# Gate and up products of a two-layer hybrid decoder: hi and lo parts of the transposed input as one 512-column operand, in blocks of 128 weight columns

## The chip, the cores and the metric

The kernel runs on one core of one Trainium2 chip. The metric is the device time of one execution in microseconds (us), lower is better. A profile is one execution recorded by the hardware profiler; its span runs from the first instruction to the last. In the profile PE is the matrix engine (TensorE), PEld its weight loads, DVE the vector engine, ACT the scalar (activation) engine, POOL the GpSimd engine and SP the engine that issues DMAs.

## What is computed

Two layers run over all 256 positions at once, with a model width of 1024 and an FFN width of 2816, all in float32. Each layer has an FFN, a mixer and a second FFN:

```python
def swiglu(x, w_gate_up, w_down):
    gate, up = jnp.split(x @ w_gate_up, 2, axis=-1)
    return (jax.nn.silu(gate) * up) @ w_down

for l in range(DEPTH):
    x = x + FFN_HALF * swiglu(rms_norm(x, ffn1_norm[l]), ffn1_w_gate_up[l], ffn1_w_down[l])
    u = rms_norm(x, mix_norm[l]) @ w_in[l]
    ...
    x = x + y @ w_out[l]
    x = x + FFN_HALF * swiglu(rms_norm(x, ffn2_norm[l]), ffn2_w_gate_up[l], ffn2_w_down[l])
return rms_norm(x, final_norm)
```

The mixer between the FFNs joins three sequence mixers (a state-space one, an mLSTM and an RWKV-7). The change does not touch its computation.

## The kernel before

**Precision by splitting.** The matrix engine works on a rounded 32-bit type (`F32R`). To keep float32 accuracy each operand is split in two: `hi` is the operand copied to `F32R`, `lo` is the rest (operand minus `hi`). A product is then three matmuls into the same bank of PSUM: hi by hi, hi by lo, lo by hi. `mm3` (lines 804 to 808) issues these three, so L806, L807 and L808 carry nearly all matrix work. Weights are split on the chip in `weights` (L773 on ACT makes hi, L774 on DVE makes lo), and activations in `split_to` (L824, L825).

**The FFN (`ffn`, line 956).** The FFN width is cut in `NG` = 11 groups of 256. The transposed, split input is held by `Turned` as two tensors, `hi` and `lo`, each 128 partitions by 8 chunks by 256 positions. Group 0 is made by `first_up` in another layout (the positions are the stationary operand and 512 weight columns move), and `turn` transposes its result. The scale of the norm comes as a row `R` from `rows`. Groups 1 to 10 are made by `gate_up` (line 1004): the weights are the stationary operand, 128 columns at a time, and the 256 positions move. For each of 8 chunks, of gate and up, and of the two halves `b` of the 256 columns one `mm3` is issued:

```python
mm3(banks[g][:, b * T:(b + 1) * T], (wh[:, k, g, b, :], wl[:, k, g, b, :]), hT(kk),
    kk == 0 and b == 0, kk == 7)
```

This is 8 x 2 x 2 x 3 = 96 matmuls of 256 columns for a group, into two banks of 512 columns. Then five steps on 512 columns follow: gate times R (L1025, DVE), Silu (L1026, ACT), times up (L1027, DVE), and the split (L824 ACT, L825 DVE). Between two groups stands `down` (line 1030) for the group before: per block of 128 FFN rows and per half `t` of the positions, 2 x 3 matmuls with 512 moving weight columns, that is 24 for a group, into four banks kept through the whole FFN (`acc`). In the last group `down` is done for positions 0 to 127 first; the next stage's `tile(0)` starts from them (residual add L834, squares L838, transposes L870 and their splits L873, L874, or L865 with L824, L825 before a mixer), while the other half's products run.

**Weights.** They come in pieces of 128 partitions by 1024 floats (512 KB), in the order of `specs`: for each FFN group four pieces of gate and up columns (`spec_gu`, each two DMAs, rows of 256 floats, 1 KB) and two pieces of down rows (`spec_rows`, rows of 4 KB). The mixer's `spec_cols` pieces have rows of 128 floats, 512 bytes.

**What sets the order.** Every operation is first recorded and then placed by a list scheduler (`Planner`, lines 158 to 587), which emits a fixed order per engine. `cost` (line 292) gives each operation an estimated occupancy; for `F32R` matmuls it is 0.46 ns per moving column. `run` (line 358) takes the operation that can start earliest; on PE the recorded order of the dense matmuls breaks ties. It assigns places in SBUF and the eight PSUM banks; three classes of bank have caps: `acc` 4, `main` 3 (gate and up, projections, transposes of the input), `task` 5 (the mixers' own). Pieces of weights are split early when their first use is near.

Of the kernel before, what the change touches and what calls it, by code (L numbers as in the profile page):

```python
# [21 lines left out]
F32 = mybir.dt.float32  # L22
# [135 lines left out]
class Planner:  # L158
# [133 lines left out]
    def cost(self, op, outs, ins):  # L292
# [65 lines left out]
    def run(self, reserve, wmin, wmax, urgent, keep_max, spare):  # L358
# [232 lines left out]
def kernel(ctx: ExitStack, tc: tile.TileContext, x, pvec, prow, fnorm, w_gate,  # L591
# [256 lines left out]
    class Turned:  # L848


        def __init__(self):
            self.hi, self.lo = (newr(8 * T).rearrange("p (k t) -> p k t", k=8) for _ in range(2))

        def __call__(self, k, t=None):
            ts = slice(0, T) if t is None else slice(t * 128, (t + 1) * 128)
            return self.hi[:, k, ts], self.lo[:, k, ts]

        def fill(self, t, src, gain=None):

            ts = slice(t * 128, (t + 1) * 128)  # L860
            if gain is None:
                for h in range(2):
                    bv = mmb().rearrange("p (k c) -> p k c", k=4)
                    for k in range(4):
                        pe.transpose(bv[:, k, :], src(h)[:, k * 128:(k + 1) * 128], ident)  # L865
                    split_to(self.hi[:, h * 4:h * 4 + 4, ts], self.lo[:, h * 4:h * 4 + 4, ts], bv)
                return
            bv = [b.rearrange("p (k c) -> p k c", k=4) for b in (mmb(), mmb())]
            for k in range(8):
                pe.transpose(bv[k % 2][:, k // 2, :], src(k // 4)[:, k % 4 * 128:(k % 4 + 1) * 128], ident)  # L870
            for k in range(8):
                v, g = bv[k % 2][:, k // 2, :], gain[:, k:k + 1]
                act.activation(out=self.hi[:, k, ts], in_=v, func=AF.Copy, scale=g)  # L873
                dve.scalar_tensor_tensor(out=self.lo[:, k, ts], in0=v, scalar=g, in1=self.hi[:, k, ts].bitcast(F32),  # L874
                                         op0=ALU.mult, op1=ALU.subtract)

    class ToFfn:

# [77 lines left out]
    def ffn(inp, update, make_next, first=None):  # L956
# [2 lines left out]
        pts = {}  # L959
        hT = inp.hT  # L960

        def pt_pair(j):
            pts[j] = newr(512), newr(512)
            return pts[j]

        def gated(ps, s, p, t):

# [16 lines left out]
        def turn(p):  # L984
            with ranked(1):
                b = mmb()
                bv = b.rearrange("p (k t c) -> p k t c", k=2, t=2)
                for t in range(2):
                    for k in range(2):
                        pe.transpose(bv[:, k, t, :], p[:, t * 256 + k * 128:t * 256 + (k + 1) * 128], ident)  # L990
                split_to(*pt_pair(0), b)

        def rows():

# [8 lines left out]

        def gate_up(j, R):

            banks = [mmb(), mmb()]
            for i in range(4):
                (w,) = weights(1)
                wh, wl = (v.rearrange("p (k g b c) -> p k g b c", k=2, g=2, b=2) for v in w[1:])
                with dense(w):  # L1010
                    for k in range(2):
                        kk = 2 * i + k
                        for g in range(2):
                            for b in range(2):

                                mm3(banks[g][:, b * T:(b + 1) * T], (wh[:, k, g, b, :], wl[:, k, g, b, :]), hT(kk),
                                    kk == 0 and b == 0, kk == 7)
            with ranked(1):
                s = new(512)
                hi, lo = pt_pair(j)  # L1020
                gate, up, sv, hv, lv = (v.rearrange("p (b c) -> p b c", b=2) for v in (*banks, s, hi, lo))
                for ts in ((slice(0, T),) if j < NG - 1 else (slice(0, 128), slice(128, T))):
                    n = ts.stop - ts.start
                    v = sv[:, :, ts]
                    dve.tensor_tensor(out=v, in0=gate[:, :, ts], in1=R[:, None, ts].to_broadcast([128, 2, n]), op=ALU.mult)  # L1025
                    act.activation(out=v, in_=v, func=AF.Silu)  # L1026
                    dve.tensor_tensor(out=v, in0=up[:, :, ts], in1=v, op=ALU.mult)  # L1027
                    split_to(hv[:, :, ts], lv[:, :, ts], v)

        def down(j, k, t, w, hs=(0, 1)):  # L1030
            hi, lo = pts[j]
            o = (k * 2 + t) * 128
            with dense(w):
                for h in hs:
                    mm3(acc[t][h], (hi[:, o:o + 128], lo[:, o:o + 128]),
                        (w[1][:, h * 512:(h + 1) * 512], w[2][:, h * 512:(h + 1) * 512]),
                        j == 0 and k == 0, j == NG - 1 and k == 1)

        p = first_up()
        if first is not None:  # L1040
            first()
        R = rows()
        for j in range(1, NG):
            gate_up(j, R)
            if acc is None:
                acc = [[accb(), accb()], [accb(), accb()]]
            if j == 1:
                turn(p)
            if j < NG - 1:
                for k in range(2):  # L1050
                    (w,) = weights(1)
                    down(j - 1, k, 0, w)
                    down(j - 1, k, 1, w)
            else:
                wa = weights(2)
                for k in range(2):
                    down(j - 1, k, 0, wa[k])
                wb = weights(2)
                for h in range(2):
                    for k in range(2):  # L1060
                        down(j, k, 0, wb[k], (h,))
                nxt = make_next()
                nxt.tile(0, (acc[0], inp.half[0]))
                for hs in nxt.tail:
                    for k in range(2):
                        down(j - 1, k, 1, wa[k], hs)
                    for k in range(2):
                        down(j, k, 1, wb[k], hs)
        return nxt, (acc[1], inp.half[1])


# [832 lines left out]
```

## Time and profile before

| what | value |
|---|---|
| time, median of 3 runs (lowest, highest) | 1304.84 us (1300.2, 1305.63) |
| profiled execution, its own time | 1305.16 us |
| its span, mean granted clock of PE | 1303.4 us, 0.990 |
| matmuls in it | 9170 |
| weight loads' busy share (PEld) | 88% |
| DVE, ACT, POOL busy share | 62%, 49%, 7% |
| DMA traffic | 210.35 MB, mean 161 GB/s |

How to read it: a matmul's duration in the profile reaches from its start to the modelled end of its pipeline, so that consecutive matmuls overlap in time and a busy PE need not be a PE at its peak. What a matmul costs in a dense stream is the distance from its start to the next one's start, called its pitch here. Busy times of a group of rows are unions, so overlapping records are not counted twice.

### The profile page before, as it was taken

What the parts mean: (1) busy time and instruction counts of PE and PEld (TensorE: products, weight loads), DVE (VectorE), ACT (ScalarE), POOL (GpSimd) and SP (SyncE); (2) the same over time, 40 slices, a digit from 0 to 9 for tenths busy, and PEclk for the clock granted to TensorE, in tenths of its full rate; (3) what the DMA queues carried; (4) which work ended last, traced back from release to release, by engine and by line L of the source; (5) the groups of instructions that cost most, each with busy time, mean ns of one, the idle gap of its engine ahead of it and who ended that gap; (6) DMA issues with size and microseconds to landing.
All of it is one profiled execution on the core that took longest, in us unless ns stands there. A gap on an engine that the chain in (4) does not pass through costs nothing.

```text
span 1303.4 us, 22885 instructions
## 1 busy us (share of the span) xinstructions
PE 1263.1 (97%) x9170; PEld 1150.5 (88%) x9170; DVE 807.2 (62%) x1154; ACT 643.4 (49%) x993; POOL 86.1 (7%) x161
## 2 busy tenths in 40 slices
PE   7999999988999999999999999999899999999997
PEld 6999997988897889999889999889799888899996
DVE  7655546985599465555475555669846993755553
ACT  7444426667464364444363344465565652634332
POOL 2000002110011010000010000111200110000001
PEclk9999999999999999999999999999999999999999
DMA  9955665052257475566374656550522674855500
GB/s 327 338 190 175 203 161 146 18 129 44 66 167 256 159 258 178 163 194 195 129 241 151 206 193 178 146 130 2 138 49 66 211 242 130 271 171 189 192 19 33
DMA packets 199962, 210.35 MB, mean 161 GB/s; under 512 B 23856, under 2 KB 175280, under 8 KB 199856
## 3 DMA queue, kind: packets, MB, share of 16 engines
q1 hardware_dynamic: 199856, 208.89, 51.6%
q8 instruction: 72, 1.18, 0.4%
q14 instruction: 34, 0.28, 0.1%
HBM read 207.01 MB, written 1.84 MB: 160 GB/s over the span
## 4 chain that ended last, share of the span: by engine, by line
PE 87%; DVE 7%; ACT 3%; issue 1%; SPq 1%; DMA 1%; POOLq 0%; DVEq 0%; POOL 0%; ACTq 0%
PE bank L806 25%; PE bank L808 25%; PE bank L807 25%; PE bank L1369 2%; DVE region L774 1%; SPq L1277 1%; PE bank L1727 1%; ACT region L773 1%; DVE region L1243 1%; PE bank L1420 1%; DVE region L1134 1%; PE bank L1415 1%; PE bank L1429 1%; PE bank L870 1%; PE bank L1584 1%
## 5 line engine op out<-in xcount | busy, mean ns | idle before, releaser
L806 PE MATMUL bank<-region,region 128*128 128x256 f32 (+1 forms) x2384 | 749.5, 315 | 2.3 <-DVE region L1243 0.9
L807 PE MATMUL bank<-region,region 128*128 128x256 f32 (+1 forms) x2384 | 748.3, 314 | 0.0
L808 PE MATMUL bank<-region,region 128*128 128x256 f32 (+1 forms) x2384 | 747.8, 314 | 0.3 <-DVE region L825 0.3
L806 PEld LDWEIGHTS bank<-region,region 128*128 128x128 f32 x2384 | 456.6, 192 | 30.8 <-DVE region L1243 1.3
L808 PEld LDWEIGHTS bank<-region,region 128*128 128x128 f32 x2384 | 456.9, 192 | 28.0 <-issue 1.5
L807 PEld LDWEIGHTS bank<-region,region 128*128 128x128 f32 x2384 | 456.7, 192 | 27.9 <-issue 2.9
L774 DVE TENSOR_TENSOR region<-region,region 128x1024 fp32r<-128x1024 f32 (+1 forms) x382 | 443.8, 1207 | 23.7 <-ACT region L773 22.7
L773 ACT ACTIVATE region<-region 128x1024 fp32r<-128x1024 f32 (+1 forms) x382 | 375.1, 1039 | 17.6 <-ACT region L773 8.4
L1025 DVE TENSOR_TENSOR region<-bank,region 128x512 f32<-128x512 f32 (+1 forms) x44 | 27.9, 642 | 269.2 <-PE bank L808 269.1
L1026 ACT ACTIVATE region<-region 128x512 f32<-128x512 f32 (+1 forms) x44 | 25.7, 593 | 329.6 <-DVE region L1025 329.6
L1134 DVE SCALAR_TENSOR_TENSOR region<-bank,pv,region 128x255 f32<-128x255 f32 (+2 forms) x84 | 39.9, 480 | 27.0 <-ACT region L1132 23.6
L824 ACT ACTIVATE region<-region 128x512 fp32r<-128x512 f32 (+1 forms) x48 | 28.1, 596 | 43.0 <-DVE region L1027 42.8
L838 ACT ACTIVATE region<-res 128x512 f32<-128x512 f32 x28 | 17.6, 627 | 63.9 <-DVE res L834 60.9
L842 POOL TENSOR_SCALAR smalls<-smalls 128x1 f32<-128x1 f32 x14 | 5.7, 406 | 622.3 <-ACT region L838 622.0
L825 DVE TENSOR_TENSOR region<-region,region 128x512 fp32r<-128x512 f32 (+1 forms) x48 | 30.5, 646 | 25.8 <-ACT region L824 25.8
L824 ACT ACTIVATE region<-bank 128x512 fp32r<-128x512 f32 x28 | 16.4, 596 | 31.9 <-PE bank L1146 13.7
L874 DVE SCALAR_TENSOR_TENSOR region<-bank,pv,region 128x128 fp32r<-128x128 f32 x64 | 19.4, 346 | 15.1 <-ACT region L873 7.5
L1027 DVE TENSOR_TENSOR region<-bank,region 128x512 f32<-128x512 f32 (+1 forms) x44 | 27.6, 635 | 0.2 <-ACT region L1026 0.2
L834 DVE SCALAR_TENSOR_TENSOR res<-bank,res 128x512 f32<-128x512 f32 x8 | 5.3, 686 | 35.1 <-PE bank L808 35.1
L1557 ACT ACTIVATE region<-bank,region 128x128 f32<-128x128 f32 x80 | 23.4, 378 | 5.8 <-PE bank L1553 3.0
L873 ACT ACTIVATE region<-bank,pv 128x128 fp32r<-128x128 f32 x64 | 20.2, 364 | 11.0 <-PE bank L870 6.3
L825 DVE TENSOR_TENSOR region<-bank,region 128x512 fp32r<-128x512 f32 x28 | 18.7, 684 | 8.9 <-ACT region L824 8.7
(290 smaller groups left out, 846.3 us busy)
## 6 DMA issues: line engine op xcount, KB each, us to landing
region<-in_f_gu_dram SPq DMA_DIRECT2D x352, 256.0 KB, 5.0
region<-in_f_dn_dram SPq DMA_DIRECT2D x88, 512.0 KB, 5.7
region<-in_w_in_dram SPq DMA_DIRECT2D x80, 512.0 KB, 4.9
region<-in_w_out_dram SPq DMA_DIRECT2D x32, 512.0 KB, 5.2
region<-in_prow_dram SPq DMA_DIRECT2D x4, 512.0 KB, 4.7
region<-in_prow_dram SPq DMA_DIRECT2D x6, 256.0 KB, 3.9
region<-in_w_gate_dram SPq DMA_DIRECT2D x2, 512.0 KB, 5.0
dn<-region SPq DMA_DIRECT2D x64, 4.0 KB, 1.5
```

Of the source, the lines that this page charges most:

```text
L773: act.activation(out=hi[:, c], in_=src[:, c], func=AF.Copy)
L774: dve.tensor_tensor(out=lo[:, c], in0=src[:, c], in1=hi[:, c].bitcast(F32), op=ALU.subtract)
L806: pe.matmul(o, lhsT=ah, rhs=bh, start=start, stop=False, skip_group_check=True)
L807: pe.matmul(o, lhsT=ah, rhs=bl, start=False, stop=False, skip_group_check=True)
L808: pe.matmul(o, lhsT=al, rhs=bh, start=False, stop=stop, skip_group_check=True)
L824: act.activation(out=hi, in_=src, func=AF.Copy)
L825: dve.tensor_tensor(out=lo, in0=src, in1=hi.bitcast(F32), op=ALU.subtract)
L1025: dve.tensor_tensor(out=v, in0=gate[:, :, ts], in1=R[:, None, ts].to_broadcast([128, 2, n]), op=ALU.mult)
L1026: act.activation(out=v, in_=v, func=AF.Silu)
L1027: dve.tensor_tensor(out=v, in0=up[:, :, ts], in1=v, op=ALU.mult)
L1134: dve.scalar_tensor_tensor(out=dst[:, s:T], in0=ps[:, 0:T - s], scalar=col(cw + 3 - s), in1=dst[:, s:T], op0=ALU.mult, op1=ALU.add)
L1369: pe.matmul(bv[q, n, :], lhsT=lhs(q, i * 8 + n), rhs=rhs(q, i * 8 + n), start=True, stop=True)
```

## The change

The input's two parts are laid side by side, so that for each chunk the 256 positions of hi and the 256 of lo are one operand of 512 columns (`both`). The stationary hi weights then need one matmul of 512 columns instead of two of 256; its first half holds hi by hi, its second hi by lo. The lo weights times hi add into the second half. The two halves of the bank are added when it is read. A bank of 512 columns thus holds one block of 128 weight columns, no longer two, and gate and up are made in 20 blocks of 128 columns, each followed by the down products of a block two earlier. The pieces of weights follow that order: four chunks by gate and up by 128 columns, rows of 512 bytes, and one piece of down rows after every two. The planner's matmul cost becomes (columns + 32) / 2.4 ns, and the cap of the `main` banks rises from 3 to 4.

```diff
             elif view(ins[0]).dtype == F32R:
-                op.occ = 0.46 * nn
+                op.occ = (nn + 32) / 2.4
...
-        caps = {"acc": 4, "main": 3, "task": 5}
+        caps = {"acc": 4, "main": 4, "task": 5}
...
+    def spec_gu_block(w, c0):
+
+        for k0 in (0, 4):
+            def dma(raw, k0=k0):
+                v = raw.rearrange("p (k g c) -> p k g c", k=4, g=2)
+                for g in range(2):
+                    src = w[k0 * 128:(k0 + 4) * 128, g * FF + c0:g * FF + c0 + 128]
+                    sp.dma_start(out=v[:, :, g, :], in_=src.rearrange("(k p) c -> p k c", p=128))
+            specs.append(dma)
+
     def spec_ffn(gu, dn):
         spec_gu(gu, 0)
         for j in range(1, NG):
-            spec_gu(gu, j)
-            spec_rows(dn, (j - 1) * 256)
+            for k in range(2):
+                spec_gu_block(gu, j * 256 + k * 128)
+                spec_rows(dn, (j - 1) * 256 + k * 128, 1)
         spec_rows(dn, (NG - 1) * 256)
...
-            self.hi, self.lo = (newr(8 * T).rearrange("p (k t) -> p k t", k=8) for _ in range(2))
+
+            self.parts = [newr(8 * T).rearrange("p (k s t) -> p k s t", k=4, s=2) for _ in range(2)]
...
+        def both(self, k):
+            return self.parts[k // 4][:, k % 4].rearrange("p s t -> p (s t)")
...
         def gate_up(j, R):
 
+
             banks = [mmb(), mmb()]
-            for i in range(4):
+            for i in range(2):
                 (w,) = weights(1)
-                wh, wl = (v.rearrange("p (k g b c) -> p k g b c", k=2, g=2, b=2) for v in w[1:])
+                wh, wl = (v.rearrange("p (k g c) -> p k g c", k=4, g=2) for v in w[1:])
                 with dense(w):
-                    for k in range(2):
-                        kk = 2 * i + k
+                    for k in range(4):
+                        kk = 4 * i + k
                         for g in range(2):
...
+                            o = banks[g]
+                            if kk < 7:
+                                pe.matmul(o, lhsT=wh[:, k, g, :], rhs=hT.both(kk), start=kk == 0, stop=False,
+                                          skip_group_check=True)
+                            pe.matmul(o[:, T:], lhsT=wl[:, k, g, :], rhs=hT(kk)[0], start=False, stop=False,
+                                      skip_group_check=True)
+                            if kk == 7:
+                                pe.matmul(o, lhsT=wh[:, k, g, :], rhs=hT.both(kk), start=False, stop=True,
+                                          skip_group_check=True)
             with ranked(1):
-                s = new(512)
-                hi, lo = pt_pair(j)
...
+                s, u = new(T), new(T)
+                hi, lo = pt_pair(j, 1)
+                gate, up = banks
+                for ts in ((slice(0, T),) if j < 2 * NG - 1 else (slice(0, 128), slice(128, T))):
+                    t2_ = slice(T + ts.start, T + ts.stop)
+                    act.activation(out=s[:, ts], in_=gate[:, t2_], func=AF.Copy)
+                    act.activation(out=u[:, ts], in_=up[:, t2_], func=AF.Copy)
+                    dve.tensor_tensor(out=s[:, ts], in0=gate[:, ts], in1=s[:, ts], op=ALU.add)
+                    dve.tensor_tensor(out=s[:, ts], in0=s[:, ts], in1=R[:, ts], op=ALU.mult)
+                    act.activation(out=s[:, ts], in_=s[:, ts], func=AF.Silu)
+                    dve.tensor_tensor(out=u[:, ts], in0=up[:, ts], in1=u[:, ts], op=ALU.add)
+                    dve.tensor_tensor(out=s[:, ts], in0=u[:, ts], in1=s[:, ts], op=ALU.mult)
+                    split_to(hi[:, ts], lo[:, ts], s[:, ts])
...
+        last = 2 * NG - 1
+        for j in range(2, 2 * NG):
             gate_up(j, R)
             if acc is None:
                 acc = [[accb(), accb()], [accb(), accb()]]
                 turn(p)
-            if j < NG - 1:
...
+            if j < last - 1:
+                (w,) = weights(1)
+                down(j - 2, 0, w)
+                down(j - 2, 1, w)
             else:
...
+                ws[j - 2] = weights(1)[0]
+                down(j - 2, 0, ws[j - 2])
+        for j in (last - 1, last):
+            ws[j] = weights(1)[0]
+        for h in range(2):
+            for j in (last - 1, last):
+                down(j, 0, ws[j], (h,))
+        nxt = make_next()
+        nxt.tile(0, (acc[0], inp.half[0]))
+        for hs in nxt.tail:
+            for j in range(last - 3, last + 1):
+                down(j, 1, ws[j], hs)
         return nxt, (acc[1], inp.half[1])
```

More of the change, by code (lines that the diff above doesn't have):

```diff
@@ L851, in __init__ @@
         def __init__(self):
-            self.hi, self.lo = (newr(8 * T).rearrange("p (k t) -> p k t", k=8) for _ in range(2))
+            self.parts = [newr(8 * T).rearrange("p (k s t) -> p k s t", k=4, s=2) for _ in range(2)]
         def __call__(self, k, t=None):
             ts = slice(0, T) if t is None else slice(t * 128, (t + 1) * 128)
-            return self.hi[:, k, ts], self.lo[:, k, ts]
+            return tuple(self.parts[k // 4][:, k % 4, s, ts] for s in range(2))
+        def both(self, k):
+            return self.parts[k // 4][:, k % 4].rearrange("p s t -> p (s t)")
         def fill(self, t, src, gain=None):
@@ L872, in fill @@
                 v, g = bv[k % 2][:, k // 2, :], gain[:, k:k + 1]
-                act.activation(out=self.hi[:, k, ts], in_=v, func=AF.Copy, scale=g)
-                dve.scalar_tensor_tensor(out=self.lo[:, k, ts], in0=v, scalar=g, in1=self.hi[:, k, ts].bitcast(F32),
-                                         op0=ALU.mult, op1=ALU.subtract)
+                hi, lo = self(k, t)
+                act.activation(out=hi, in_=v, func=AF.Copy, scale=g)
+                dve.scalar_tensor_tensor(out=lo, in0=v, scalar=g, in1=hi.bitcast(F32), op0=ALU.mult, op1=ALU.subtract)
     class ToFfn:
@@ L960, in ffn, with pt_pair @@
         hT = inp.hT
-        def pt_pair(j):
-            pts[j] = newr(512), newr(512)
-            return pts[j]
+        def pt_pair(j, n):
+            both = newr(n * 512)
+            hi, lo = both[:, 0:n * 256], both[:, n * 256:]
+            for k in range(n):
+                pts[j + k] = hi[:, k * 256:(k + 1) * 256], lo[:, k * 256:(k + 1) * 256]
+            return hi, lo
         def gated(ps, s, p, t):
@@ L990, in turn @@
                         pe.transpose(bv[:, k, t, :], p[:, t * 256 + k * 128:t * 256 + (k + 1) * 128], ident)
-                split_to(*pt_pair(0), b)
+                split_to(*pt_pair(0, 2), b)
         def rows():
@@ L1013, in gate_up @@
                         for g in range(2):
-                            for b in range(2):
-                                mm3(banks[g][:, b * T:(b + 1) * T], (wh[:, k, g, b, :], wl[:, k, g, b, :]), hT(kk),
-                                    kk == 0 and b == 0, kk == 7)
-            with ranked(1):
-                s = new(512)
-                hi, lo = pt_pair(j)
[L1021 to L1028, printed above, removed]
@@ L1033, in down @@
+        def down(j, t, w, hs=(0, 1)):
+            hi, lo = (v[:, t * 128:(t + 1) * 128] for v in pts[j])
             with dense(w):
                 for h in hs:
-                    mm3(acc[t][h], (hi[:, o:o + 128], lo[:, o:o + 128]),
-                        (w[1][:, h * 512:(h + 1) * 512], w[2][:, h * 512:(h + 1) * 512]),
-                        j == 0 and k == 0, j == NG - 1 and k == 1)
+                    mm3(acc[t][h], (hi, lo), (w[1][:, h * 512:(h + 1) * 512], w[2][:, h * 512:(h + 1) * 512]),
+                        j == 0, j == 2 * NG - 1)
@@ L1039, in ffn @@
+        ws = {}
         p = first_up()
@@ L1042, in ffn @@
         R = rows()
-        for j in range(1, NG):
+        last = 2 * NG - 1
+        for j in range(2, 2 * NG):
             gate_up(j, R)
@@ L1046, in ffn @@
                 acc = [[accb(), accb()], [accb(), accb()]]
-            if j == 1:
                 turn(p)
-            if j < NG - 1:
[L1050 to L1053, printed above, removed]
-            else:
[L1055 to L1068, printed above, removed]
+            if j < last - 1:
+                (w,) = weights(1)
+                down(j - 2, 0, w)
+                down(j - 2, 1, w)
+            else:
+                ws[j - 2] = weights(1)[0]
[10 more added lines that the diff above has]
+                down(j, 1, ws[j], hs)
         return nxt, (acc[1], inp.half[1])
```

5 lines of the change are left out of this document (1 added, 4 removed).

## The prediction, on record before the result

> **What bounds the kernel now.** I first read the page: busy times, the slices, and the chain of work that ended last.
>
> ```profile
> PE 1263.1 (97%) x9170; PEld 1150.5 (88%) x9170; DVE 807.2 (62%) x1154; ACT 643.4 (49%) x993; POOL 86.1 (7%) x161
> PEclk9999999999999999999999999999999999999999
> PE 87%; DVE 7%; ACT 3%; issue 1%; SPq 1%; DMA 1%; POOLq 0%; DVEq 0%; POOL 0%; ACTq 0%
> PE bank L806 25%; PE bank L808 25%; PE bank L807 25%; PE bank L1369 2%; DVE region L774 1%; SPq L1277 1%; PE bank L1727 1%; ACT region L773 1%; DVE region L1243 1%; PE bank L1420 1%; DVE region L1134 1%; PE bank L1415 1%; PE bank L1429 1%; PE bank L870 1%; PE bank L1584 1%
> ```
>
> Three quarters of the chain are the three lines of `mm3`, at the full granted clock. Next the table by stretches: from left, the stretch, its length, busy us (and instructions) of PE, PEld, DVE, ACT and POOL, the clock, the DMA share and GB/s. The rows are the first FFN's inside, the first mixer with its ends, the second FFN's inside and the second mixer.
>
> ```profile
> 22.00:198.00 176.00, 176.00 (x1231) 165.18 (x1230) 98.29 (x118) 77.68 (x95) 5.46 (x19) 1.00 0.70 219
> 198.00:458.00 260.00, 247.39 (x1987) 220.01 (x1985) 189.70 (x317) 144.63 (x256) 29.57 (x47) 0.98 0.42 123
> 474.00:650.00 176.00, 175.97 (x1231) 164.93 (x1230) 93.74 (x100) 73.93 (x90) 0.19 (x1) 1.00 0.56 181
> 842.00:1102.00 260.00, 248.71 (x1984) 220.38 (x1982) 188.32 (x316) 144.50 (x255) 28.53 (x47) 0.98 0.42 123
> ```
>
> Inside an FFN PE never rests, while DVE works 93.74 of 176 us, ACT 73.93 and the DMA engines 56%. What a matmul costs in the stream sets the time there, and nothing else. That is the stage which the change touches.
>
> **What a matmul costs.** I read the pitch from the starts in PE's timeline, for the group that goes from 505.48 to 522.46 us: 24 matmuls of 512 columns (`down`), then 96 of 256.
>
> ```profile
> 505.48 0.40 PE L806 MATMUL bank<-region,region 128*128 128x512 f32 x1
> 505.71 0.40 PE L807 MATMUL bank<-region,region 128*128 128x512 f32 x1
> 506.64 0.39 PE L808 MATMUL bank<-region,region 128*128 128x512 f32 x1
> 510.95 0.28 PE L806 MATMUL bank<-region,region 128*128 128x256 f32 x1
> 511.06 0.28 PE L807 MATMUL bank<-region,region 128*128 128x256 f32 x1
> 522.46 0.40 PE L806 MATMUL bank<-region,region 128*128 128x512 f32 x1
> ```
>
> The 256-column matmul: (522.46 - 510.95) / 96 = 119.9 ns. The 512-column one, from the sixth of its run on: (510.95 - 506.64) / 19 = 226.8 ns. Twice 119.9 is 239.8, so a matmul carries 239.8 - 226.8 = 13.0 ns that do not grow with its columns. The first five of the run are dearer: (506.64 - 505.48) / 5 = 232 ns, 26 ns in all above 226.8. Of this about 7 come back at the other end, where 510.95 to 511.06 is 0.11 us. So a round trip between the sizes costs about 20 ns.
>
> **The change, part by part.** *Matmuls.* A chunk of gate or of up for 128 weight columns took three matmuls of 256, 359.7 ns. It now takes one of 512 and one of 256, 226.8 + 119.9 = 346.7 ns. That saves 13.0 ns. There are 8 chunks x 2 x 20 blocks = 320 such pairs in an FFN and 1280 in four: 16.7 us saved. The columns streamed stay the same, so only the fixed part is won; PE has 1280 fewer matmuls of its 9170. `first_up`, `down` and the mixers keep theirs. Weight loads: a load's pitch is that of its matmul, and at 119.9 ns a load still fits behind each, so the load for the 512 one fits behind the 256 one ahead of it.
>
> *Alternating sizes.* No row shows 512 and 256 taking turns. From above, a pair could pay the whole round trip, 20 ns; from below, it could get the 7 ns at the return without paying the start, a gain. I take 0, by the rows nearest to one pair: the first 512 after a 256 takes 505.48 to 505.71, 230 ns, and the first 256 after a 512 takes 110, together 340, not above 346.7. The down run is now cut in two for each old group, one more round trip: 40 x 20 ns = 0.8 us lost.
>
> The Trainium skill's page "TensorE: Matmul & The Clock Gate", section "Back-to-back issue gap", puts the fixed part of an isolated warm matmul at 2.5 ns, N / 2.4 + 2.5, which speaks against most of this gain. By it the pairs would save 1280 x 2.5 ns = 3.2 us, an estimate. The trace does not agree: that formula gives 109.2 ns for 256 columns where 119.9 were measured, and 215.8 for 512 where 226.8 were.
>
> *Evacuation.* These rows give the prices, at 512, 256 and 128 columns, and that of a split of weights (L774).
>
> ```profile
> L1025 DVE TENSOR_TENSOR region<-bank,region 128x512 f32<-128x512 f32 x36 | 24.9, 692 | 239.5 <-PE bank L808 239.4
> L1026 ACT ACTIVATE region<-region 128x512 f32<-128x512 f32 x36 | 22.8, 633 | 294.6 <-DVE region L1025 294.6
> L969 DVE TENSOR_TENSOR region<-bank,region 128x256 f32<-128x256 f32 x8 | 3.4, 419 | 0.6 <-ACT region L968 0.6
> L1001 ACT ACTIVATE region<-bank 128x256 f32<-128x256 f32 x4 | 1.5, 377 | 0.4 <-PE bank L998 0.4
> L1026 ACT ACTIVATE region<-region 128x256 f32<-128x256 f32 x8 | 2.9, 414 | 35.0 <-DVE region L1025 35.0
> L774 DVE TENSOR_TENSOR region<-region,region 128x1024 fp32r<-128x1024 f32 (+1 forms) x382 | 443.8, 1207 | 23.7 <-ACT region L773 22.7
> L873 ACT ACTIVATE region<-bank,pv 128x128 fp32r<-128x128 f32 x64 | 20.2, 364 | 11.0 <-PE bank L870 6.3 <-DVE region L874 4.3
> L874 DVE SCALAR_TENSOR_TENSOR region<-bank,pv,region 128x128 fp32r<-128x128 f32 x64 | 19.4, 346 | 15.1 <-ACT region L873 7.5 <-PE bank L870 7.4
> ```
>
> Before, a group took 3 DVE steps of 692 ns, 2.1 us, and 2 ACT steps of 633, 1.3 us. Now two blocks take 10 DVE steps of 419, 4.2 us, and 8 ACT steps, 2 x (2 x 377 + 2 x 414) ns = 3.2 us. In ten groups DVE rises by 21 us to some 115 of 172 us in an FFN, ACT by 19 to 93. The work that hides it is PE's dense stream: a block's result is used two blocks later, behind a block of gate and up (16 x 346.7 ns = 5.5 us) and 12 down products (2.7 us), against a chain of 3 ACT and 4 DVE steps, 2.9 us and its hand-overs. With a pair of banks in use and a pair being read, the four `main` banks suffice. I cost it at nothing there. Without that cover a block would wait for the whole chain.
>
> *The last block of an FFN*, where the next stage starts, has less cover. In the last FFN the first DVE step, the first down product, the first step of lo and the first product of the last two blocks are these:
>
> ```profile
> 1284.65 0.76 DVE L1025 TENSOR_TENSOR region<-bank,region 128x256 f32<-128x256 f32 x2 [8.28 <-PE bank L808]
> 1285.16 0.40 PE L806 MATMUL bank<-region,region 128*128 128x512 f32 x1
> 1286.46 0.76 DVE L825 TENSOR_TENSOR region<-region,region 128x256 fp32r<-128x256 f32 x2 [0.16 <-ACT region L824]
> 1287.91 0.61 PE L806 MATMUL bank<-region,region 128*128 128x512 f32 x2
> ```
>
> The first half was ready at 1286.46 + 0.42 = 1286.88 and used at 1287.91, 1.0 us to spare. The new chain of seven steps of 346 to 364 ns is 2.5 us and 0.2 of hand-overs, and gate's bank, whose last matmul starts 227 + 120 + 227 ns = 0.57 us before the first down product and lasts 0.40, is complete 0.2 us before it, where the first step began 0.5 before it. It is ready about 2.5 us after that product's start. The cover that is certain is 9 products, 9 x 226.8 = 2.0 us; 12 if the planner reorders, 2.7. So 0 to 0.5 us is lost at each of four ends; I take 1 us in all.
>
> *The first down products* need `turn`, which had a whole group as cover and now has one block, 5.5 us.
>
> ```profile
> 23.29 0.28 PE L806 MATMUL bank<-region,region 128*128 128x256 f32 x1
> 29.42 0.68 DVE L825 TENSOR_TENSOR region<-bank,region 128x512 fp32r<-128x512 f32 x1
> 476.77 0.28 PE L806 MATMUL bank<-region,region 128*128 128x256 f32 x1
> 480.21 0.69 DVE L825 TENSOR_TENSOR region<-bank,region 128x512 fp32r<-128x512 f32 x1 [2.25 <-ACT region L824]
> ```
>
> In the second FFN it ends 4.1 us after gate and up began, in time. In the first it ends 6.8 us after, 1.3 late, unless PE does the next block meanwhile: 0 to 1.3 us, I take 0.5.
>
> *Weights.* Each group still has six pieces of 512 KB and ten DMAs on SP's queue; only their order and rows change. Rows of 512 bytes are shown by the projections' pieces (second row), rows of 1 KB by the first.
>
> ```profile
> 30.00:40.00 10.00, 10.00 (x67) 9.11 (x66) 8.96 (x11) 4.65 (x7) 0.00 (x0) 1.00 1.07 364
> 160.00:168.00 8.00, 8.00 (x69) 8.00 (x69) 3.66 (x4) 2.95 (x3) 0.00 (x0) 1.00 1.11 278
> ```
>
> With the engines full they move 278 GB/s instead of 364. PE asks for six pieces, 3.1 MB, in some 16.6 us: 190 GB/s. No cost, and none at the start either, where pieces arrive every 1.9 us and are used every 2.8.
>
> *Planner.* A new matmul cost (120 for 118 ns at 256 columns, 227 for 235 at 512) and the fourth `main` bank reorder the mixers too. Their rows above leave PE 12.6 and 11.3 us of rest, and one wait differs between the two layers, 7.4 us in two times, the longest 4.6:
>
> ```profile
> PE bank L1575 <- DVE region L1543: 7.4, 2, 4.6
> ```
>
> So one plan differs from the next by some 1.8 us at one place; in a mixer I allow 4 us either way and take 0.
>
> **Sum.** -16.7 + 0.8 + 1 + 0.5 = -14.4 us. The profiled execution took 1305.16 us with a span of 1303.4 us, 0.3 us above the median of the runs, so the difference carries over: 1304.84 - 14.4 = 1290.4 us.
>
> **Rivals.** A measurement of this kernel can tell about 0.5%, 6.5 us, from no change.
>
> *A: as summed, 1290.4 us*, by itself 1284 to 1297 with the ends' bounds and the mixers' plans. For it: the period of the group is just 24 and 96 pitches and 0.02 us. Chance 0.73.
>
> *B: alternating sizes pays a toll in every pair.* Place: each 512 after a 256 in `gate_up`. Price: 1.28 us for each ns of toll. From 14.4 / 1.28 = 11 ns on the kernel is slower; at the whole 20 ns it takes 1290.4 + 25.6 = 1316 us. For it: the five dear starts of every run. Against it: the first of them is among the cheap ones, and the return gives it back. Chance 0.10, 0.06 of it beyond 16.4 ns, where it is slower by over 0.5%, and 0.04 below.
>
> *C: the mixers' plan comes out worse*, since four `main` banks and four left for tasks meet work that had five. Up to 8 us: 1298. For it: they hold all the waits of PE that are left. Against it: two layers that are placed differently last equally long, 260 us of the same windows with 247.39 and 248.71 busy. Chance 0.09, in thirds of faster, no change and slower by more (0.03, 0.04, 0.02).
>
> *D: the fixed part is not saved*, as it goes with columns: by the planner's old 0.46 ns per column a 512 takes 235.5 ns, and the pair 355.4, 4.3 ns less than three: 5.5 us less 2.3 lost, 1301.6 us. By the 2.5 ns of the Trainium skill's page above it would be 1304 us. Against it: the 226.8. Chance 0.03.
>
> *E: DVE and ACT hold PE*: their steps sit between the splits of weights (1.2 us each on DVE) in strict order, and if each of 76 blocks waited 0.1 us, 7.6 us would be lost: 1298. Against it: 67% of DVE. Chance 0.05 (0.02, 0.02, 0.01).
>
> **How the numbers follow.** Faster by over 0.5% (under 1298.3): 0.73 + 0.03 + 0.02 = 0.78. Within: 0.04 + 0.04 + 0.03 + 0.02 = 0.13. Slower (over 1311.4): 0.06 + 0.02 + 0.01 = 0.09. The range of 8 in 10 is A's own with C, D and part of B: 1283 to 1302.
>
> **What would show it.** In the new profile: 7890 matmuls; in PE's timeline inside an FFN, starts that alternate by 227 and 120 ns, 346.7 for a pair; 16.6 us for two blocks with their down products; DVE near 115 and ACT near 93 us busy in an FFN, with no idle PE in front of `down`; FFN stretches shorter by about 4 us each, and mixers unchanged within 4. Pairs above 358 ns would make it wrong by B; equal pairs with a longer mixer by C.

## The result, and the profile after

The changed kernel takes 1297.74 us (median of 5 runs, 1294.27 to 1297.86), the kernel before 1304.46 us in the runs beside it (median of 5, 1300.2 to 1305.63). The ratio is 0.9949 with a 95% interval of 0.9928 to 0.997: some 6.7 us faster, where 14.4 were forecast. The profiled execution took 1296.8 us with a span of 1294.9 us.

These are the busy times, the shares of the chain that ended last, and the first row of the DMA issues, from the page of the changed kernel.

```profile
PE 1249.7 (97%) x7890; PEld 1077.5 (83%) x7890; DVE 894.7 (69%) x1442; ACT 715.1 (55%) x1241; POOL 90.1 (7%) x161
...
PE 85%; DVE 6%; ACT 3%; DMA 2%; SPq 1%; issue 1%; POOL 0%; POOLq 0%; DVEq 0%; ACTq 0%
PE bank L1036 20%; PE bank L819 13%; PE bank L818 13%; PE bank L817 13%; PE bank L1038 12%; PE bank L1041 3%; PE bank L1393 1%; DVE region L785 1%; PE bank L1751 1%; DMA region<-in_f_gu_dram 1%; DMA region<-dn 1%; ACT region L784 1%; PE bank L1444 1%; PE bank L1453 1%; PE bank L1608 1%
```

The three lines of `mm3` are now L817 to L819. L1036 is the new matmul of 512 columns, L1038 the one of 256 with the lo weights, L1041 the 512 of the last chunk, which comes after its 256. Exactly 1280 matmuls are gone, and PE still holds 85% of the chain. The table by stretches, in the columns of the prediction's, shows the insides of the first and the second FFN:

```profile
22.00:190.00 168.00, 167.55 (x882) 142.40 (x881) 115.67 (x184) 91.65 (x150) 7.16 (x17) 1.00 0.81 232
474.00:640.00 166.00, 166.00 (x876) 141.79 (x874) 111.15 (x159) 87.92 (x139) 0.00 (x0) 1.00 0.67 197
```

In the second FFN PE never rests, with DVE at 67% and ACT at 53%. So whatever is missing there lies in the pitch of the matmuls. PE's timeline in that FFN (start, duration, instruction) gives it; a block of gate and up goes from 536.07 us to the last row, where the next down products begin.

```profile
533.34 0.39 PE L817 MATMUL bank<-region,region 128*128 128x512 f32 x1
...
536.07 0.39 PE L1036 MATMUL bank<-region,region 128*128 128x512 f32 x1
536.29 0.28 PE L1038 MATMUL bank<-region,region 128*128 128x256 f32 x1
536.41 0.40 PE L1036 MATMUL bank<-region,region 128*128 128x512 f32 x1
536.64 0.28 PE L1038 MATMUL bank<-region,region 128*128 128x256 f32 x1
536.76 0.40 PE L1036 MATMUL bank<-region,region 128*128 128x512 f32 x1
537.00 0.28 PE L1038 MATMUL bank<-region,region 128*128 128x256 f32 x1
...
540.65 0.40 PE L1036 MATMUL bank<-region,region 128*128 128x512 f32 x1
541.71 0.39 PE L817 MATMUL bank<-region,region 128*128 128x512 f32 x1
```

From 536.41 to 540.65 us stand 12 pairs: 4.24 / 12 = 353.3 ns each, where 346.7 were forecast. A pair thus pays 6.6 ns more than its two pitches. The block with its down products takes 541.71 - 533.34 = 8.37 us.

Where the rest of the time is, the starts of the stages show. A mixer begins with the first transposes after an FFN, and so does an FFN after a mixer. In the kernel before, these two rows bound the second FFN:

```profile
457.41 0.27 PE L870 MATMUL bank<-ident,res 128*128 128x128 f32 x1
...
648.38 0.38 PE L870 MATMUL bank<-ident,res 128*128 128x128 f32 x2
```

In the changed kernel, the first row starts the first mixer, and the other two bound the second FFN:

```profile
199.41 0.33 PE L880 MATMUL bank<-ident,region 128*128 128x128 f32 x1 [1.67 <-DVE region L933]
...
458.08 0.38 PE L885 MATMUL bank<-ident,res 128*128 128x128 f32 x2
...
646.97 0.38 PE L885 MATMUL bank<-ident,res 128*128 128x128 f32 x2
```

The second FFN went from 190.97 to 188.89 us. Taken in the same way, from each profile's starts, all stages are (the last FFN with the end of the kernel):

| us | FFN | mixer | FFN | FFN | mixer | FFN | four FFNs | two mixers |
|---|---|---|---|---|---|---|---|---|
| before | 196.2 | 256.4 | 191.0 | 196.1 | 256.7 | 202.2 | 785.5 | 513.1 |
| after | 195.1 | 258.7 | 188.9 | 193.7 | 254.2 | 200.0 | 777.8 | 512.9 |

The FFNs gained 7.7 us, where 14.4 were forecast, and the mixers 0.2 in sum.

### The profile page after: what moved, and what is told of

Read it like the earlier page. It is cut to its first block, busy times and chain, and to the rows that moved or that the text cites. A ratio compares the mean times of both kernels' runs of the same rounds, so it can differ in the third digit from the quotient of the medians.

```text
span 1294.9 us, 20867 instructions
## 1 busy us (share of the span) xinstructions
PE 1249.7 (97%) x7890; PEld 1077.5 (83%) x7890; DVE 894.7 (69%) x1442; ACT 715.1 (55%) x1241; POOL 90.1 (7%) x161
## 4 chain that ended last, share of the span: by engine, by line
PE 85%; DVE 6%; ACT 3%; DMA 2%; SPq 1%; issue 1%; POOL 0%; POOLq 0%; DVEq 0%; ACTq 0%
PE bank L1036 20%; PE bank L819 13%; PE bank L818 13%; PE bank L817 13%; PE bank L1038 12%; PE bank L1041 3%; PE bank L1393 1%; DVE region L785 1%; PE bank L1751 1%; DMA region<-in_f_gu_dram 1%; DMA region<-dn 1%; ACT region L784 1%; PE bank L1444 1%; PE bank L1453 1%; PE bank L1608 1%
## 5 line engine op out<-in xcount | busy, mean ns | idle before, releaser
L1036 PE MATMUL bank<-region,region 128*128 128x512 f32 x1120 | 398.2, 398 | 0.0
L817 PE MATMUL bank<-region,region 128*128 128x512 f32 (+1 forms) x1104 | 386.7, 350 | 0.5 <-DVE region L1267 0.4
L818 PE MATMUL bank<-region,region 128*128 128x512 f32 (+1 forms) x1104 | 384.7, 349 | 0.0
L819 PE MATMUL bank<-region,region 128*128 128x512 f32 (+1 forms) x1104 | 384.1, 349 | 0.5 <-DVE region L836 0.5
L1038 PE MATMUL bank<-region,region 128*128 128x256 f32 x1280 | 346.5, 281 | 0.0
L1036 PEld LDWEIGHTS bank<-region,region 128*128 128x128 f32 x1120 | 210.4, 188 | 50.9
L1038 PEld LDWEIGHTS bank<-region,region 128*128 128x128 f32 x1280 | 241.6, 189 | 6.5
L819 PEld LDWEIGHTS bank<-region,region 128*128 128x128 f32 x1104 | 210.1, 190 | 27.9 <-DVE region L836 1.5
L818 PEld LDWEIGHTS bank<-region,region 128*128 128x128 f32 x1104 | 210.0, 190 | 25.9 <-issue 0.5
L817 PEld LDWEIGHTS bank<-region,region 128*128 128x128 f32 x1104 | 210.1, 190 | 25.7 <-issue 1.3
L1049 ACT ACTIVATE region<-bank 128x256 f32<-128x256 f32 (+1 forms) x84 | 30.9, 373 | 220.2 <-PE bank L1041 220.2
L1051 DVE TENSOR_TENSOR region<-bank,region 128x256 f32<-128x256 f32 (+1 forms) x84 | 34.2, 410 | 127.0 <-ACT region L1049 127.0
L836 DVE TENSOR_TENSOR region<-region,region 128x256 fp32r<-128x256 f32 (+2 forms) x88 | 36.9, 424 | 35.6 <-ACT region L835 35.6
L1053 ACT ACTIVATE region<-region 128x256 f32<-128x256 f32 (+1 forms) x84 | 34.0, 408 | 49.3 <-DVE region L1052 49.3
L1041 PE MATMUL bank<-region,region 128*128 128x512 f32 x160 | 60.2, 399 | 0.0
L835 ACT ACTIVATE region<-region 128x256 fp32r<-128x256 f32 (+2 forms) x88 | 36.2, 416 | 37.4 <-DVE region L1055 37.0
L1055 DVE TENSOR_TENSOR region<-region 128x256 f32<-128x256 f32 (+1 forms) x76 | 32.0, 422 | 10.9 <-ACT region L1053 2.4
```

Of the source, the lines that this page charges most:

```text
L817: pe.matmul(o, lhsT=ah, rhs=bh, start=start, stop=False, skip_group_check=True)
L818: pe.matmul(o, lhsT=ah, rhs=bl, start=False, stop=False, skip_group_check=True)
L819: pe.matmul(o, lhsT=al, rhs=bh, start=False, stop=stop, skip_group_check=True)
L835: act.activation(out=hi, in_=src, func=AF.Copy)
L836: dve.tensor_tensor(out=lo, in0=src, in1=hi.bitcast(F32), op=ALU.subtract)
L1036: pe.matmul(o, lhsT=wh[:, k, g, :], rhs=hT.both(kk), start=kk == 0, stop=False, skip_group_check=True)
```

## The experiments

Two theories stood at the start. *Toll:* a switch of size costs time in every pair. *Rest:* the pairs are as cheap as forecast, or cannot be made cheaper, and the difference is in the plan, the evacuation or the ends. The expectations call this 'plan', and name a third, 'operand': the time belongs to the 256-column matmul into half a bank or to the doubled operand, wherever it stands. Each experiment is an edit of the changed kernel, but for `e5_plan_only`, which edits the kernel before. All ratios are to the kernel before, run beside it. The code is shown in part.

**Same sizes together** (`e1_sorted`). The same matmuls in another order; the second piece has the 256s first.

```diff
-                    for k in range(4):
-                        for g in range(2):          # 512, 256, 512, 256, ...
+                    for lo, k, g in [(s, k, g) for s in ((1, 0) if i else (0, 1))
+                                     for k in range(4) for g in range(2)]:
```

> The changed kernel with the same matmuls in another order: in the first piece of a block's weights all eight 512-column ones and then all eight 256-column ones, in the second piece the reverse, so that a 512 follows a 256 once in a block instead of 15 times (the planner's matmul cost is (columns + 33) / 2.4, so that it finds a plan). Theory 'toll' (a 512 that follows a 256 starts late, about 6 ns a pair, 7.8 us in all): in runs a 512 takes 227 ns and a 256 120, a block of gate and up with its 12 down products takes 8.30 us instead of 8.38, and the kernel 1290 to 1292 us. Rival 'operand' (the toll belongs to the 256-column matmul into half a bank or to the doubled operand, wherever it stands): two kinds together stay at 353 ns, 1297 to 1298 us. Rival 'plan' (the gain was lost in the mixers and at stage ends): FFN stretches as in the changed kernel, 1295 to 1300 us.

Measured: 1289.07 us (median of 6), ratio 0.9903 [0.988, 0.9925]. PE's timeline between two blocks' down products, and the starts that bound the second FFN:

```profile
530.19 0.39 PE L817 MATMUL bank<-region,region 128*128 128x512 f32 x1
...
534.72 2.08 PE L1035 MATMUL bank<-region,region 128*128 128x256 f32 x16
536.63 2.00 PE L1038 MATMUL bank<-region,region 128*128 128x512 f32 x8
538.48 0.39 PE L817 MATMUL bank<-region,region 128*128 128x512 f32 x1
```

```profile
455.50 0.27 PE L885 MATMUL bank<-ident,res 128*128 128x128 f32 x1
...
643.18 0.38 PE L885 MATMUL bank<-ident,res 128*128 128x128 f32 x2
```

Sixteen 256s in a run take 1.91 us, 119.4 ns each, and a block 8.29 us instead of 8.37. The second FFN takes 187.7 us, 1.2 less than in the changed kernel; the four FFNs 770.8 us, 7.0 less, with mixers of 512.5 us, near the 512.9 of the changed kernel. In the FFNs' work nothing but the order differs. The planner's cost is not quite the same: (columns + 33) / 2.4 here, in `e3_runs4` and in `e8_lo384`. But `e6_sorted_oldplan` and `e7_oldplan` below differ in the order alone, and their FFNs take 772.1 and 778.4 us, 6.3 apart. So the toll comes with the order, and its size is shown.

Sorting also changes which bank follows which: a pair writes the same bank twice in a row, while the sorted runs take gate's and up's bank in turn. `e4_three` below writes one bank three times in a row at 119.8 ns a matmul, without a toll, so a repeated bank alone costs nothing. Whether it adds to the price of a switch is not shown.

**Shorter runs** (`e2_runs2`, `e3_runs4`). The two 512s of a chunk, then its two 256s; and two chunks taken together, runs of four. The lines are shown against `e1_sorted`; as there, the last run of a block has its 256s first.

```diff
-                    for lo, k, g in [... for s in (0, 1) for k in range(4) for g in range(2)]:
+                    for lo, k, g in [... for r in range(0, 4, n) for s in (0, 1)     # n = 1; n = 2
+                                     for k in range(r, r + n) for g in range(2)]:
```

> The changed kernel with gate's and up's matmuls of a chunk sorted: two of 512 columns, then two of 256 (seven or eight switches in a block instead of 15). Theory 'toll', if every switch costs the same 6 ns: 45 ns a block instead of about 100, 4 us less than the changed kernel, 1293 to 1294 us. Toll growing with the run, as the dear starts of the kernel before suggest (7 and 9 ns of excess for the first two, 7 given back): 9 ns a switch, 2 to 3 us less, 1295 us. Rivals 'operand' and 'plan': no change, 1297 to 1298 us.

> The same with two chunks sorted together: runs of four, three switches in a block (planner's cost with 33). 'Toll' with the same 6 ns for every switch: 19 ns a block, 6.5 us under the changed kernel, 1291 us; growing with the run (17 ns for a run of four, 20 for the last): 54 ns a block, 4 us under it, 1293 to 1294 us. Rivals: 1297 to 1298 us.

Measured: `e2_runs2` 1287.52 us (4), ratio 0.9886 [0.9863, 0.9909]; `e3_runs4` 1289.75 us (4), ratio 0.9904 [0.9881, 0.9927]. The starts of two consecutive blocks' down products, first with runs of two, then with runs of four:

```profile
533.65 0.39 PE L817 MATMUL bank<-region,region 128*128 128x512 f32 x1
...
541.96 0.39 PE L817 MATMUL bank<-region,region 128*128 128x512 f32 x1
```

```profile
538.13 0.39 PE L817 MATMUL bank<-region,region 128*128 128x512 f32 x1
...
546.45 0.39 PE L817 MATMUL bank<-region,region 128*128 128x512 f32 x1
```

The blocks take 8.31 and 8.32 us, which is also the median of the 72 whole blocks in each profile (8.37 in the changed kernel's, 8.29 in that of `e1_sorted`). The bare pitches of a block sum to 16 x 346.7 + 12 x 226.8 ns = 8.27 us. Above that stand 0.10 us when sizes alternate, 0.04 with runs of two, 0.05 with runs of four and 0.02 with the longest. A 512 follows a 256 15, 7, 3 times and once in a block. So half the switches take away more than half of the toll, and runs of four do not beat runs of two. A fixed price of 6.6 ns would give 0.05 us for runs of two, near what was measured, but 0.02 for runs of four; the toll that grows with the run hits runs of four (54 ns expected), but would give 7 x 9 ns = 0.06 us for runs of two. Neither fits both.

Both kernels came out faster than either form of 'toll' had it. Of the lower time of `e2_runs2` 6.6 us came from its mixers (506.3 us), which the order of the FFNs' matmuls does not touch; with FFNs of 773.2 us it is no better there than `e1_sorted`. `e3_runs4` has FFNs of 774.4 and mixers of 510.0 us.

**Without the wide operand** (`e4_three`). The new blocks, pieces, evacuation and plan, but three matmuls of 256 columns into the same halves.

```diff
-                            pe.matmul(o, lhsT=wh[:, k, g, :], rhs=hT.both(kk), ...)
+                            pe.matmul(o[:, :T], lhsT=wh[:, k, g, :], rhs=hi, ...)
+                            pe.matmul(o[:, T:], lhsT=wh[:, k, g, :], rhs=lo, ...)
                             pe.matmul(o[:, T:], lhsT=wl[:, k, g, :], rhs=hi, ...)
```

> The changed kernel with three 256-column matmuls in place of one of 512 and one of 256, into the same halves of the same banks: everything of the change but the wide operand. The toll is gone and so is the saving: 359.9 ns for a pair's work, 1280 x (359.9 - 352.8) ns = 9 us over the changed kernel, 1306 to 1307 us by 'toll'. What it stands above the kernel before (1304.5 us) is the price of the rest: blocks of 128, evacuation, rows of 512 bytes, plan; I expect 2 us. By 'plan' it would be 1310 us or more, as the pairs would have saved the whole 16.7 us. By 'operand' the 256-column ones into the second half would stand above 120 ns.

Measured: 1305.16 us (10), ratio 1.0021 [1.0008, 1.0034].

```profile
527.93 0.40 PE L817 MATMUL bank<-region,region 128*128 128x512 f32 x1
...
530.68 0.28 PE L1036 MATMUL bank<-region,region 128*128 128x256 f32 x1
...
536.43 0.40 PE L817 MATMUL bank<-region,region 128*128 128x512 f32 x1
```

A block takes 8.50 us, half a group of the kernel before 16.98 / 2 = 8.49, and the FFNs 786.7 us, 1.1 more than before. So everything in the FFN that comes with the wide operand (halves to add, smaller blocks, rows of 512 bytes) costs 1.1 us in this profile; with the plan it is 0.2% in the runs. All of the gain is the wide matmul's. From 530.68 us on the 48 matmuls of 256 take 5.75 us, 119.8 ns each, two thirds of them into the second half, so 'operand' falls. So does 'plan', by which 1310 us or more were expected.

**The planner's settings alone** (`e5_plan_only`), on the kernel before:

```diff
-                op.occ = 0.46 * nn
+                op.occ = (nn + 32) / 2.4
...
-        caps = {"acc": 4, "main": 3, "task": 5}
+        caps = {"acc": 4, "main": 4, "task": 5}
```

> The kernel before with only the planner's two changes (matmul cost, fourth main bank). By the reading that the FFNs hold the whole effect: the four FFN stretches last as before, 785.5 us in all, and the mixers move by up to 4 us each, 1298 to 1309 us, most likely 1304. If the planner's change by itself were a gain or a loss that the changed kernel hides, the FFN stretches or both mixers would move the same way by over 4 us.

Measured: 1306.96 us (10), ratio 1.0034 [1.0019, 1.0049]. The new settings lose 0.3% by themselves, 4 us. The stages of its one profile hold 1 us of that (FFNs 786.3, mixers 513.3, the first 3.8 us longer than before and the second 3.6 shorter). The rest lies in which executions were profiled: that of the kernel before took 1305.16 us, 2.2 above the median of its runs here (1302.92), this one 1306.09, 0.9 below its own.

**The old settings under the changed kernels** (`e6_sorted_oldplan`, `e7_oldplan`): the edit above backwards, with the sorted order and with the change's own.

> The sorted order of e1_sorted with the planner's old cost (0.46 ns a column) and three main banks. FFN stretches as in e1_sorted, 771 us in all, if the toll is all that the order changes and the planner's settings do nothing in the FFN; the mixers, 512 us there, may come out 4 us either way: 1285 to 1293 us.

> The changed kernel with the planner's old settings (0.46 ns a column, three main banks). FFN stretches as in the changed kernel, 778 us in all, since the toll stays: both readings agree there. If the planner's settings cost something of their own (the kernel before with the new ones stood 0.34% above it, the sorted order with the old ones 6.6 us under the one with the new cost), the mixers come out near the 507.3 us of e6 and the kernel at 1290 to 1293 us. If a plan is a draw that no setting governs, the mixers lie anywhere from 506 to 513 us: 1290 to 1298 us.

Measured: `e6_sorted_oldplan` 1282.48 us (4), ratio 0.9841 [0.9814, 0.9868], the fastest of all and below the range expected, as its mixers took 507.3 us; `e7_oldplan` 1292.75 us (6), ratio 0.9917 [0.9902, 0.9931]. The FFNs of `e7_oldplan` take 778.4 us, like those of the changed kernel, so the toll is there without the new plan. But its mixers take 507.6 us instead of 512.9. Its first mixer lies between these rows:

```profile
199.60 0.44 PE L880 MATMUL bank<-ident,region 128*128 128x128 f32 x2 [1.51 <-DVE region L933]
...
450.78 0.38 PE L885 MATMUL bank<-ident,res 128*128 128x128 f32 x2
```

That is 251.2 us, against 199.41 to 458.08, 258.7, in the changed kernel. The waits of PE in that stretch (total us, count, longest) are led by these, in the changed kernel and then in `e7_oldplan`:

```profile
PE bank L1363 <- DVE region L1567: 6.6, 1, 6.6
PE bank L1393 <- DMA region<-dh: 2.2, 1, 2.2
PE bank L880 <- DVE region L933: 1.7, 1, 1.7
PE bank L1393 <- DMA region<-dg: 1.2, 1, 1.2
```

```profile
PE bank L1363 <- DVE region L1567: 1.9, 1, 1.9
PE bank L1528 <- DVE region L1148: 1.6, 1, 1.6
```

One wait, at the same line for the same step of DVE, is 4.7 us shorter. The rows of the whole stretch, again for the changed kernel and then for `e7_oldplan`, have the clock in the third place from the end:

```profile
199.41:458.08 258.67, 244.39 (x1976) 217.06 (x1976) 186.48 (x313) 140.68 (x250) 27.84 (x45) 0.98 0.45 132
199.60:450.78 251.18, 242.78 (x1975) 214.70 (x1976) 187.09 (x313) 141.84 (x250) 27.45 (x45) 1.00 0.45 130
```

PE rests 14.3 us in the one and 8.4 in the other, which is 5.9 of the 7.5 us. The other 1.6 is busy time, at a granted clock of 0.98 against 1.00. The clock differs from run to run of the same kernel: beside `e1_sorted` the kernel before took 1300.1 to 1300.7 us where its mean was 0.995, and 1305.0 to 1307.6 where it was 0.990 or 0.991. So the mixers of single profiles can be compared only to a few us. The FFNs can be compared better: the first three stood at 1.00 in every profile, and the last at 0.99.

**Which of the two settings** (`e10_sorted_cap3`: new cost, three `main` banks; `e11_sorted_oldcost`: old cost, four), both sorted; and the old settings with runs of two (`e12_runs2_oldplan`). The edits are single lines of the diff above.

> The sorted order with the new matmul cost ((columns + 32) / 2.4) and three main banks: parts the planner's two changes. If the fourth bank is what costs, the mixers are near 507 us and the kernel at 1282 to 1285 us; if the new cost is, near 512 us and 1288 to 1290 us; if it is a draw, anything between. FFN stretches 771 us.

> The other half of that pair: the sorted order with the old cost and four main banks. If the fourth bank costs, 1288 to 1290 us; if the new cost does, 1282 to 1285 us. FFN stretches 771 us.

> Runs of two with the planner's old settings, one more draw of the plan: with the new ones its mixers took 506.3 us, the shortest of all. FFN stretches as there, 773 us. If the old settings are better by themselves, the mixers stay at 507 us or less, 1283 to 1287 us; if it is a draw, they can be 5 us longer, up to 1292 us.

| kernel | cost, `main` banks | us (runs) | ratio [95%] | FFNs | mixers |
|---|---|---|---|---|---|
| e1_sorted | new (with 33), 4 | 1289.07 (6) | 0.9903 [0.988, 0.9925] | 770.8 | 512.5 |
| e10_sorted_cap3 | new, 3 | 1287.21 (4) | 0.9876 [0.9857, 0.9895] | 771.9 | 511.5 |
| e11_sorted_oldcost | old, 4 | 1284.19 (4) | 0.9851 [0.9831, 0.9871] | 773.4 | 504.7 |
| e6_sorted_oldplan | old, 3 | 1282.48 (4) | 0.9841 [0.9814, 0.9868] | 772.1 | 507.3 |
| e12_runs2_oldplan | old, 3 | 1284.67 (4) | 0.9852 [0.9834, 0.9871] | 772.9 | 504.5 |

With the blocks of 128, the old cost gave mixers of 504.5 to 507.6 us in all four plans, the new one 506.3 to 512.9 in eight (the changed kernel, `e1` to `e4` and `e8` to `e10`), six of them 510 or more. In the first mixer PE rests 7.5 to 8.4 us in the four and 9.1 to 14.3 in the eight.

In each of the four pairs of kernels with the same order and another cost (in two of them the banks differ too), the old cost has the lower ratio, by 0.0032 to 0.0052, and the lower median, by 2.9 to 5.0 us. The intervals of one pair stand apart (`e11` and `e1`, which has the 33), the others touch or overlap. A line through all runs, 0.87 us for each 0.001 of granted clock, leaves 2.7 to 4.4 us of it, an estimate. So the cost matters, by some 3 to 4 us. Three banks came out 1.7 and 1.9 us below four, inside the intervals. Why a cost that is nearer to the pitches makes worse plans is not shown, nor why two of its plans (`e2` and `e8`) have mixers as short as those of the old one.

**What the toll hangs on** (`e8_lo384`, `e9_lo128`, one run each): the lo matmul made wider and narrower, in the change's alternating order. `e8` adds products that do not belong to the result, and `e9` leaves out lo by hi for half of the positions.

```diff
-                            pe.matmul(o[:, T:], lhsT=wl[:, k, g, :], rhs=hT(kk)[0], ...)
+                            pe.matmul(o[:, 128:], lhsT=wl[:, k, g, :], rhs=hT.both(kk)[:, 0:384], ...)   # e8
+                            pe.matmul(o[:, T:T + 128], lhsT=wl[:, k, g, :], rhs=hT(kk, 0)[0], ...)       # e9
```

> A look at what the toll hangs on. The changed kernel with the lo weights' matmul 384 columns wide instead of 256 (it also adds lo by half of hi into the first half, and a part of lo by lo is added to the second; the output is not the reference's). Untolled pair: 226.7 + 173.3 = 400.0 ns. If the toll comes with any change of size: 405 to 407 ns. If it comes because a 256-column matmul lasts just as long as the weight load beside it, so that loads cannot run ahead: 400 ns.

> The same look from the other side: the lo weights' matmul takes 128 columns (lo by hi is left out for positions 128 to 255). Untolled pair: 226.7 + 66.7 = 293.3 ns. If the toll comes with any change of size: about 300 ns. If the weight load is what cannot keep up behind a short matmul: up to 53 ns more, as a load then finds 67 ns where it had 120, 310 to 347 ns.

Measured: 1360.36 us and 1283.12 us, one profile each. PE's timeline, where 12 pairs lie between the first row and the last, with 384 columns and then with 128:

```profile
553.39 0.39 PE L1036 MATMUL bank<-region,region 128*128 128x512 f32 x1
553.62 0.34 PE L1038 MATMUL bank<-region,region 128*128 128x384 f32 x1
...
558.27 0.39 PE L1036 MATMUL bank<-region,region 128*128 128x512 f32 x1
```

```profile
535.09 0.45 PE L1036 MATMUL bank<-region,region 128*128 128x512 f32 x1
535.38 0.22 PE L1038 MATMUL bank<-region,region 128*128 128x128 f32 x1
...
539.18 0.44 PE L1036 MATMUL bank<-region,region 128*128 128x512 f32 x1
```

The pitches of 256 and 512 columns, 119.9 and 226.8 ns, fit (columns + 32) / 2.4 within 0.3 ns. By that line a pair with 384 would take 400.0 ns and one with 128 293.3. Measured: 4.88 / 12 = 406.7 ns and 4.09 / 12 = 340.8 ns. With 384 the toll is 6.7 ns, as good as the same, so by this one profile it does not come from the 256 columns being short beside the weight load ahead. With 128 the pair pays 47 ns, something else: halving the columns of its small matmul saved 353.3 - 340.8 = 12.5 ns of a possible 53. That a matmul cannot be shorter than the load of the next weights is a guess that fits, and was not tested.

## Why the prediction was wrong, point by point

**The step that failed** is "*Alternating sizes.* ... I take 0, by the rows nearest to one pair". Those rows were 230 ns for the first 512 after a run of 256s and 110 for the first 256 after a run of 512s. In the alternating stream the longest steps are 536.41 to 536.64 and 536.76 to 537.00, 230 and 240 ns, the return between them takes 120, not 110, and the mean pair is 353.3. Starts that are printed to 10 ns could not have shown a toll of 6.6 in two single steps anyway; it takes a mean over many pairs. What a single switch costs between long runs was no measure of what a switch costs when there are nothing but switches. The reason against rival B, "the return gives it back", fell with it. The toll of 6.6 ns is 1280 x 6.6 = 8.4 us; 0.8 of that the kernel before paid already and 0.8 stood in the sum, which leaves 6.8 us, and the FFNs fell short by 14.4 - 7.7 = 6.7. This is rival B below its turning point: its own price gives 1290.4 + 1.28 x 6.6 = 1298.8 us, and 1297.74 was measured. The sign that was set for B, pairs above 358 ns, lies where the whole gain is lost, so a pair of 353.3 did not reach it.

**The fixed part** was right. Once the order is sorted, the block goes from 8.49 to 8.29 us, 80 x 0.20 = 16 us, against 16.7 - 0.8 forecast, and the FFNs fall by 785.5 - 770.8 = 14.7 us, against 14.4. So the saving of the wide matmul is there, and the change gave half of it back by its order alone. The 2.5 ns that the prediction quoted from the Trainium skill's page "TensorE: Matmul & The Clock Gate", section "Back-to-back issue gap", given there for an isolated matmul, would have left 3.2 us, an estimate. The traces of this stream, with 16 us over the 80 blocks, do not agree.

**Evacuation** was right: DVE 111 and ACT 88 us in 166 us, the forecast shares (115 and 93 of 172), without a wait of PE. `e4_three` says the same from the other side: the FFNs with all of the extra steps and none of the saving are 1.1 us longer, 0.8 of which is the second round trip of `down`.

**Ends and the start** were small, as taken: 0.8 + 1 + 0.5 us were forecast, and `e4_three` shows 1.1 for all three together. The first down products did not wait for `turn`; these are PE's rows around them, with the one wait of that stretch ahead of them:

```profile
26.55 0.44 PE L1009 MATMUL bank<-ident,region 128*128 128x128 f32 x2 [0.45 <-DVE region L988]
...
29.77 0.40 PE L1041 MATMUL bank<-region,region 128*128 128x512 f32 x1
30.00 0.48 PE L817 MATMUL bank<-region,region 128*128 128x512 f32 x1
```

The 0.45 us is the wait of the transposes in `turn`. The first FFN gained 1.1 us where the other three gained 2.1 to 2.4; where the rest of that difference lies is not shown.

**Weights** cost nothing, as forecast: the DMA engines' share in the second FFN's inside rose from 0.56 to 0.67, and PE did not rest there.

**Mixers** were forecast unchanged within 4 us each, and were: 2.3 us longer and 2.5 shorter. That the two cancel is luck. What the prediction did not see is that with the planner's old settings the changed kernel's mixers would have taken 507.6 us (`e7_oldplan`) instead of 512.9, a part of which is the clock. Rival C had the right term, but it looked at the number of banks, which makes no difference beyond the intervals, and not at the cost.

## What to carry to other kernels

A wide operand that saves a matmul saves its fixed part, here 13 ns each, but matmuls of two sizes taking turns gave half of it back: issue those of one size together. A pitch read inside a long run, or at its edge, says nothing certain of an alternating stream, so where a gain hangs on some ns per instruction, the order itself has to be measured. And compare stage by stage: a new estimate in the planner cost the mixers, which the change does not touch, some 3 to 4 us, where the whole result was 6.7.

## What the runs showed of the hardware

Matmuls of 512 and 256 columns in turn cost 6.6 ns per pair above their two pitches, and 6.7 with 384 columns in place of 256 (one profile). Above the bare pitches, a block pays 0.10 us alternating, 0.04 in runs of two, 0.05 in runs of four and 0.02 in the longest runs. Why the toll is not in step with the number of switches stays open. In one profile a 128-column matmul beside one of 512 brought the pair only to 340.8 ns, 12.5 less than with 256 columns. The granted clock of a run, 0.990 to 0.995 in the kernel before, goes with some 5 us of its time.
